# A longer planned landing time for cache pages in the second layer of a decoder step

## The chip, the cores and the metric

The kernel runs on one core of a Trainium2 chip. A core has five engines that run side by side: PE multiplies matrices, DVE works element by element and reduces, ACT computes functions and copies, POOL does element work more slowly, and SP issues DMAs. Each takes its own instructions strictly in the order in which they stand in the program and waits on semaphores for the others. The metric is the device time of one execution in microseconds (us); lower is better. Three runs of the kernel before are given, and one more execution was profiled.

## What is computed

One inference step of a decoder with two layers, for a prompt of 512 tokens and for 8 samples of 8 new tokens each (576 columns in all), in float32. Layer 0 is a gated delta rule mixer. Between the layers, keys and values that both groups share are projected. Layer 1, the one that matters here, is differential attention. The prompt attends to itself; each sample attends to 1024 past positions, which lie in a cache of pages of 128 positions, and to its own 8 tokens. Cut to layer 1 and the cache:

```python
past = page_table.shape[1] * PAGE_SIZE                      # 8 pages of 128 for each sample
k_past = cache_k[page_table].reshape(db, past, DIFF_HEADS, 2 * DIFF_DH)
v_past = cache_v[page_table].reshape(db, past, DIFF_HEADS, DIFF_VH)

def diff_block(q, k, v, q_pos, k_pos, lam):
    s = jnp.einsum('bqhmd,bkhmd->bhmqk', q, k) * DIFF_DH ** -0.5
    s = jnp.where((k_pos[None, :] <= q_pos[:, None])[None, None, None], s, -jnp.inf)
    p = jax.nn.softmax(s, axis=-1)
    p = p[:, :, 0] - lam * p[:, :, 1]
    return jnp.einsum('bhqk,bkhe->bqhe', p, v)

def diff_mixer(...):
    q, z = jnp.split(h @ w_in, [DIFF_WIDTH], axis=-1)
    ...
    o = rms_norm(o, sub_gain) * (1.0 - lam_init)
    o = o * jax.nn.silu(z)
    return o @ w_out
```

The page table gives each of the 8 samples 8 pages, in any order among the 80 of the cache. So 64 key pages and 64 value pages are read, 512 KB each.

## The kernel before

**How the program comes about.** The source does not write its instructions down in their final order. It is a planner: each piece of work is a Python generator that yields, before each group of instructions, the engine it will use, an estimated cost, and what must be done first: names of results, or a free buffer (a `Room`). The planner (`Weave`, and `Second` for layer 1) keeps for every engine the estimated moment at which it is free. In `drive` it looks at all live pieces, takes the one that could start earliest (of equals, the one of lower rank), lets it write its instructions, and books the engine. The order thus made is the order in the program: `pin` ties PE, ACT, DVE, POOL and, in layer 1, SP to it.

DMAs are planned as well. `load` enters a transfer with an estimated time; `transfers` lets the queue run, and when a transfer is through it notes its name in `done` with a moment at which its result may be used: the end of the transfer plus `LATE` = 0.6 us. That line is the one that changes. The moment has no part in the program: on the chip each instruction waits on a semaphore for its data. It decides only which work stands ahead of which.

**The pages.** `Pages.loads` goes through 128 pages in a fixed sequence: the keys of three samples, then by turns the values of one sample and the keys of the sample three further on. There are five buffers (`PG` = 5). For each page it takes the next free buffer, has POOL copy the page number into it (L2471), has SP read that number (L2474) and issue the load (L2476). The load's name for the planner is `kpage` or `vpage` with the page's number.

**Who uses them.** `Sample2.keys` multiplies queries with the key pages on PE, two pages at a time (`px<-pg,qs` in the profile: 8 matmuls a page, which the profile records as 16), and frees each buffer after its page. `Sample2.softmax` makes the probabilities (`px<-C,sp` turns them). `Sample2.values` multiplies them with the value pages, again in pairs (`po<-pg,pTs`). In the text, key pages are k0 to k63 and value pages v0 to v63 by sample; "page 11" of a sample's values means the v page of that number.

**What stands between the pages on PE.** The attention of the prompt (`Prompt2`): for each of 8 heads, scores (`sc<-kT,qT`, with the mask `sc<-cmaskb,identb`) in three groups for four blocks of queries, then a maximum on DVE (L2709), exponentials on ACT (L2713), a combination on DVE (L2726), transposes on PE (`pt<-con_ident,pm`) and the product with the values (`pv<-vn,pts`). Further the last value projections and the z projection in tiles of 24 matmuls, 8 steps of 3 (`pq<-hhi,whi`, `pq<-hlo,whi`, `pq<-hhi,wlo`). A tile needs a bank of PSUM; ACT and DVE (L2222, L2224) empty it. The bank `pq` is there once; when the last prompt head is through, `pick` lets z tiles take `pt2`, `sc` or `pv` too.

Weights come in float32 (`wraw`), are cast on ACT (L2013) and split on POOL in two halves (L2018) into a high and a low part. After the last page come the end of the samples' attention (`samples_end`), the rest of z and the output projection (`out_second`), whose first four tiles are taken in the banks pq, px, px and po.

Line numbers of the kernel after are two higher in these places. Buffer numbers as in `pq_17438` tell one tile from the next in the same bank.

Of the kernel before, what the change touches and what calls it, by code (L numbers as in the profile page):

```python
# [253 lines left out]
class Weave:  # L254
# [76 lines left out]
    def transfers(self, until):  # L331

        while True:
            act = [q for q in self.queues.values() if q]
            rate = SHARED if len(act) > 1 else 1.0
            lands = self.clock + min(q[0][0] for q in act) / rate if act else math.inf
            comes = self.coming[0][0] if self.coming else math.inf
            t = max(self.clock, min(lands, comes))
            if t > until or t == math.inf:
                return  # L340
            for q in act:
                q[0][0] -= (t - self.clock) * rate
            self.clock = t
            if comes <= lands:
                _, _, q, us, name = self.coming.pop(0)
                self.queues[q].append([us, name])
            else:
                for q in act:
                    if q[0][0] < 1e-9:
                        self.done[q.pop(0)[1]] = t + LATE, None  # L350
                return

    def set(self, *name):
# [517 lines left out]
LATE = 0.6  # L871
# [30 lines left out]
LATER_ROOMS = "z", "z", "v", "scr", "scr"  # L902
LATER_AT = 3
SB = 3
HELD = 4
EV = 3
CH = 3
# [1115 lines left out]
def run_part(W, K, j, ps, half, ks, step=2, conds=lambda k: ()):  # L2023

    ks = list(ks)
    for i in range(0, len(ks), step):
        now = ks[i:i + step]
        yield "E", None, ("w", j), *[c for k in now for c in conds(k)]
        w = W.sets[j]
        for k in now:  # L2030
            for a, b in ((0, 0), (0, 1), (1, 0)):
                K.mm(out=ps[:, :HT], lhsT=w[a][:, k, :], rhs=(K.hhi, K.hlo)[b][:, k, half * HT:half * HT + HT],
                     start=(k == 0 and a + b == 0), stop=(k == 7 and a == 1))
# [750 lines left out]
def out_second(W, K):  # L2784
# [31 lines left out]
    def conds(half):  # L2816
        return lambda k: (("g", k, half),) + ((("gs", 1),) if half else ())
    held = []
    names = ["pq", "px", "px", "po", "sc", "sc", "pt2", "pv"]
    for (m, half), name in zip(order[:HELD], names):  # L2820
        yield None, 0, Room(name), *((("gs", 1),) if name in ("px", "po") else ())
        bank = getattr(K, name).tile([128, 512], F32, name=name), W.took[0]
        yield from run_part(W, K, 40 + m, bank[0], half, range(7), conds=conds(half))
        held.append(bank)
    for (m, half), bank in zip(order[:HELD], held):
        yield from run_part(W, K, 40 + m, bank[0], half, (7,), conds=conds(half))
        W.add(0, evac(m, half, bank))
        if half:
            W.leave(W.sets[40 + m][2])
    for i, (m, half) in enumerate(order[HELD:]):  # L2830
        name = names[(i + HELD) % 8]
        yield None, 0, Room(name)
# [125 lines left out]
def phase_b(K, ctx, past):  # L2958
# [4 lines left out]
    def pool(name, bufs):  # L2963
        return ctx.enter_context(tc.tile_pool(name=name, bufs=bufs))
# [6 lines left out]
    K.pg = pool("bpg", PG)  # L2971
    K.scr = pool("scr", SB)
    first = pool("b1", 1)
# [21 lines left out]
    K.wnext -= 1  # L2995
    for name, bufs in (("pp", 3), ("pt", 2), ("px", 2), ("po", 1), ("pg", PG), ("scr", SB), ("ch", CH), ("vch", EV), ("tk", 2), ("raw", 2),
                       ("w", 4), ("w2", 3), ("wx", 1), ("qs", 2), ("p", PB), ("pTs", 2), ("os", 1), ("C", 2), ("ls", 2), ("mx", 2),
# [205 lines left out]
```

## Time and profile before

| what | us |
|---|---|
| three runs | 1198.29, 1199.89, 1205.4 |
| median of the runs | 1199.89 |
| the profiled execution | 1203.46 |
| its span, first to last instruction | 1201.7 |
| first use of a key page on PE | at 835.8 |
| first use of a value page | at 900.8 |
| last use of a value page | begins at 1092.3 |

A row of the profile names a line of the source, an engine, an operation and the tiles it writes and reads. In a timeline the first two numbers are start and duration, then follows, in brackets, how long the engine sat idle before and what ended that. Matmuls are pipelined: their durations overlap, so what one costs PE is the distance from its start to the start of the next. A stretch by windows gives for each engine the busy time and the number of instructions, then the clock granted to PE (1.00 is full), the share of time in which the DMA engines were busy, and GB/s. In the list of waits a row says who waited for whom, how long in all, how often, and the longest.

### The profile page before, as it was taken

To read this page: it belongs to the slowest core of one execution; us is meant where nothing else is said; L and a number is where in the kernel's file an instruction comes from. 1 tells how busy PE (TensorE), PEld (TensorE's weight loads), DVE (VectorE), ACT (ScalarE), POOL (GpSimd) and SP (SyncE) were. 2 spreads that over 40 slices of the span, in tenths; PEclk is the share of its full clock that TensorE was granted. 3 is DMA by queue.
4 is the path that set the end of the run, shared out by engine and by line. 5 is a ranking of instruction groups with operands and counts; after the bars stand their busy time and mean duration, and the time that the engine had idled before them with its cause. 6 is when DMAs were issued, how large, how long until landed. Compare 5 with 4: busy or idle time off the path is not lost.

```text
span 1201.7 us, 33311 instructions
## 1 busy us (share of the span) xinstructions
PE 1147.5 (95%) x12819; PEld 1050.2 (87%) x12819; DVE 766.7 (64%) x2223; ACT 688.0 (57%) x1894; POOL 373.8 (31%) x720
## 2 busy tenths in 40 slices
PE   8999999999999999899989999999999999998998
PEld 6899899998989998899988989998997777777998
DVE  5667876767877876668635467487644555555542
ACT  4766768677776867576545243865435545543430
POOL 2432322241322323232122340656524223121241
PEclk8999999999999999999999999999999999999999
DMA  9786667676666566566958985322948998993243
GB/s 363 211 216 161 156 158 165 178 168 185 175 175 174 135 173 153 179 176 172 255 164 232 337 283 181 106 66 79 346 154 310 326 334 304 346 329 100 58 125 116
DMA packets 87935, 241.06 MB, mean 201 GB/s; under 512 B 14482, under 2 KB 28690, under 8 KB 87778
## 3 DMA queue, kind: packets, MB, share of 16 engines
q1 hardware_dynamic: 71650, 180.22, 43.4%
q0 software_dynamic: 16128, 58.73, 22.2%
q8 instruction: 101, 1.65, 0.6%
q14 instruction: 56, 0.46, 0.1%
HBM read 213.07 MB, written 25.84 MB: 199 GB/s over the span
## 4 chain that ended last, share of the span: by engine, by line
PE 61%; DMA 14%; ACT 8%; issue 7%; DVE 6%; POOL 2%; SPq 1%; POOLq 0%; DVEq 0%; ACTq 0%
PE pp L292 16%; PE pp L1922 10%; PE pc L292 6%; DMA whi<-wall 5%; PE px L1922 5%; PE pq L1922 5%; PE pt L292 3%; PE sc L1922 3%; PE pt L1922 2%; DMA pg<-cv 2%; PE pt L1927 2%; PE po L1922 2%; PE pa L292 2%; PE pv L1922 2%; DMA pg<-ck 2%
## 5 line engine op out<-in xcount | busy, mean ns | idle before, releaser
L2018 POOL TENSOR_TENSOR wlo<-wraw,whi 128x512 fp32r<-128x512 f32 x94 | 122.8, 1327 | 179.0 <-ACT whi L2013 169.4
L292 PE MATMUL pp<-hlo,whi 128*128 128x288 f32 x592 | 172.3, 311 | 0.0
L292 PE MATMUL pp<-hhi,whi 128*128 128x288 f32 x592 | 163.1, 296 | 0.0
L1922 PE MATMUL pp<-hhi,whi 128*128 128x288 f32 x432 | 132.5, 307 | 3.0 <-DVE x L1821 2.3
L1922 PE MATMUL pp<-hlo,whi 128*128 128x288 f32 x432 | 127.6, 296 | 2.0 <-DVE hlo L1847 1.6
L1922 PE MATMUL pp<-hhi,wlo 128*128 128x288 f32 x432 | 125.9, 296 | 0.9 <-POOL wlo L2018 0.6
L292 PE MATMUL pp<-hhi,wraw 128*128 128x288 f32 x576 | 124.8, 301 | 0.0
L292 PEld LDWEIGHTS pp<-hlo,whi 128*128 128x128 f32 x592 | 112.3, 190 | 1.9 <-issue 1.2
L292 PEld LDWEIGHTS pp<-hhi,whi 128*128 128x128 f32 x592 | 112.5, 190 | 0.6
L292 PE MATMUL pp<-hhi,wlo 128*128 128x288 f32 x592 | 104.1, 303 | 0.1
L292 PEld LDWEIGHTS pp<-hhi,wraw 128*128 128x128 f32 x576 | 94.6, 190 | 0.5
L1922 PEld LDWEIGHTS pp<-hhi,whi 128*128 128x128 f32 x432 | 81.4, 188 | 6.6 <-issue 5.3
L1128 DVE SCALAR_TENSOR_TENSOR y<-u,vec,y 128x600 f32<-128x600 f32 x96 | 82.9, 865 | 5.6 <-ACT y L1125 5.1
L292 PEld LDWEIGHTS pp<-hhi,wlo 128*128 128x128 f32 x592 | 84.7, 188 | 2.0 <-issue 1.2
L292 PE MATMUL pp<-hlo,wraw 128*128 128x288 f32 x288 | 84.3, 315 | 0.0
L1922 PEld LDWEIGHTS pp<-hlo,whi 128*128 128x128 f32 x432 | 81.5, 189 | 2.7 <-DVE hlo L1847 2.1
L1922 PEld LDWEIGHTS pp<-hhi,wlo 128*128 128x128 f32 x432 | 80.7, 188 | 1.3 <-POOL wlo L2018 0.8
L937 POOL DMA_DIRECT2D wlo<-wall x38 | 33.7, 887 | 125.8 <-ACT wlo L932 84.9
L2471 POOL COPY pg<-ptt 1x1 int32<-1x1 int32 x128 | 25.8, 206 | 142.3 <-PE px L1922 78.4
L2013 ACT CAST whi<-wraw 128x1024 fp32r<-128x1024 f32 x47 | 49.0, 1046 | 33.8 <-DMA wraw<-wall 9.5
L1922 PE MATMUL pq<-hhi,whi 128*128 128x288 f32 x192 | 61.8, 322 | 3.1 <-DVE x L2224 2.9
L1922 PE MATMUL pq<-hhi,wlo 128*128 128x288 f32 x192 | 57.1, 297 | 0.0
(512 smaller groups left out, 3150.8 us busy)
## 6 DMA issues: line engine op xcount, KB each, us to landing
pg<-ck SPq DMA_DIRECT2D x64, 512.0 KB, 5.4
pg<-cv SPq DMA_DIRECT2D x64, 512.0 KB, 5.2
wraw<-wall SPq DMA_DIRECT2D x49, 512.0 KB, 4.4
whi<-wall POOLq DMA_DIRECT2D x38, 512.0 KB, 6.3
wlo<-wall POOLq DMA_DIRECT2D x38, 512.0 KB, 6.0
wraw<-wall POOLq DMA_DIRECT2D x36, 512.0 KB, 5.9
araw<-ada SPq DMA_DIRECT2D x24, 512.0 KB, 5.2
araw<-ada SPq DMA_DIRECT2D x8, 1024.0 KB, 14.6
```

The source lines that it names most:

```text
L292: return self.K.nc.tensor.matmul(**kw)
L937: K.nc.gpsimd.dma_start(out=lo[:], in_=src, accum_op=ALU.add)
L1128: nc.vector.scalar_tensor_tensor(out=y[:, :YW], in0=u[:, j:j + YW], scalar=cw[j], in1=y[:, :YW], op0=ALU.mult, op1=ALU.add)
L1922: return self.K.nc.tensor.matmul(**kw)
L1927: return self.K.nc.tensor.transpose(**kw)
L2013: nc.scalar.copy(out=hi[:], in_=raw[:])
L2018: nc.gpsimd.tensor_sub(out=lo[:, q:q + 4], in0=raw[:, q:q + 4], in1=hi[:, q:q + 4].bitcast(F32))
L2471: nc.gpsimd.tensor_copy(out=e, in_=P.ptt[0:1, i:i + 1])
```

## The change

One constant is new, and the moment of use that `transfers` notes depends on the name of what landed. For a name that holds "page" it is the end of the transfer plus `SPARE` = 1.4 us, for all others plus `LATE` = 0.6 us as before. Only the loads of layer 1's cache pages have such names.

```diff
             else:
                 for q in act:
                     if q[0][0] < 1e-9:
-                        self.done[q.pop(0)[1]] = t + LATE, None
+                        name = q.pop(0)[1]
+                        self.done[name] = t + (SPARE if "page" in str(name[0]) else LATE), None
                 return
...
 SB = 3
+SPARE = 1.4
 HELD = 4
```

Each engine has as many instructions as before; one of the 16 z tiles takes the bank `pt2` where `sc` was taken. The order on PE is the same until the key pages are in use, and differs from there to the end of the z projection. The places that the prediction speaks of are shown there.

## The prediction

> **What bounds the kernel now.** I read the page first (busy shares, then the chain that ended last), then busy time by stage, then who waits for whom on PE in the paged stage, then PE's timeline there row by row. The page's busy row and its chain by engine:
>
> ```profile
> PE 1147.5 (95%) x12819; PEld 1050.2 (87%) x12819; DVE 766.7 (64%) x2223; ACT 688.0 (57%) x1894; POOL 373.8 (31%) x720
> PE 61%; DMA 14%; ACT 8%; issue 7%; DVE 6%; POOL 2%; SPq 1%; POOLq 0%; DVEq 0%; ACTq 0%
> ```
>
> PE is nearly always busy, so a reordering that adds no work can win only PE's waits. The change acts where cache pages are used. Three stretches (PE, PEld, DVE, ACT and POOL busy, then clock, DMA share, GB/s): the last key pages, the stage that mixes value pages, keys, prompt attention and the z projection, and the tail after the last page.
>
> ```profile
> 865.00:900.00 35.00, 35.00 (x411) 33.87 (x410) 13.55 (x44) 13.48 (x26) 9.36 (x29) 1.00 0.51 178
> 900.00:1092.00 192.00, 183.89 (x2680) 146.36 (x2682) 100.79 (x303) 100.53 (x292) 48.99 (x139) 1.00 0.91 320
> 1092.00:1202.00 110.00, 100.61 (x744) 95.99 (x744) 51.44 (x132) 32.79 (x78) 29.19 (x22) 0.98 0.29 87
> ```
>
> Before 900 PE does not idle at all; from 900 to 1092 it idles 8.1 us, in the tail 9.4 us. Its waits, in the paged stage and then in the tail (us in all, times, longest):
>
> ```profile
> PE po L1922 <- DMA pg<-cv: 4.0, 7, 1.2
> PE px L1922 <- DMA pg<-ck: 1.6, 3, 0.7
> PE po L1922 <- POOL pg L2471: 0.8, 2, 0.4
> PE px L1922 <- POOL pg L2471: 0.6, 1, 0.6
> ...
> PE pq L1922 <- DVE x L2224: 2.6, 2, 2.3
> PE px L1922 <- DVE hlo L2665: 2.2, 1, 2.2
> ```
>
> The first four rows are all waits for a page (POOL's copy is a step of the same load): 4.0 + 1.6 + 0.8 + 0.6 = 7.0 us in 13 waits of about half a us. A page's loop is: PE ends with a buffer, POOL copies the page number, SP issues, the page lands, PE uses it. One step of it from the trace, issue to landing of the 128 pages:
>
> ```profile
> DMA to landing us min/median/max: 3.7/5.2/8.0
> ```
>
> With a copy of 0.17 us and about 1 us until SP issues it, a page takes some 6.5 us from release to landing. There are five buffers, so what decides is the PE work that the order puts between the last use of page n-5 and the first use of page n.
>
> **The change, part by part.** It adds no instruction to any engine. It tells the planner that a page lands 1.4 us after its transfer instead of 0.6, so a page's use sorts 0.8 us later and other ready PE work goes ahead of it. Loads of weights keep 0.6. The order is the same up to the key pages and differs from there to the last projection.
>
> First place, PE around value pages 12 to 15 of the second sample. Before (po<-pg is a pair of pages; pt2 transposes values, px<-C turns probabilities):
>
> ```order
> L1922 MATMUL po<-pg,pTs 8x128 x16
> L1927 MATMUL pt_14403<-con_ident,vch 128x128 x4
> L1922 MATMUL px<-C,sp 128x64 x8
> L1927 MATMUL pt_14451<-con_ident,vch 128x128
> L1922 MATMUL po<-pg,pTs 8x128 x16
> ```
>
> Now, from that last single transpose to the same pair:
>
> ```order
> L1929 MATMUL pt_14457<-con_ident,vch 128x128
> L1924 MATMUL sc<-kT,qT 128x128 x2
> L1924 MATMUL sc<-kT,qT 128x256 x2
> L1924 LDWEIGHTS identb
> L1924 MATMUL sc<-cmaskb,identb 128x128
> L1924 LDWEIGHTS identb
> L1924 MATMUL sc<-cmaskb,identb 128x128
> L1924 LDWEIGHTS identb
> L1924 MATMUL sc<-cmaskb,identb 128x128
> L1924 LDWEIGHTS identb
> L1924 MATMUL sc<-cmaskb,identb 128x128
> L1924 MATMUL po<-pg,pTs 8x128 x16
> ```
>
> A group of prompt scores moved ahead of the pair; one pair earlier, four k steps of z instead of two follow pages 10 and 11, and the score group of 512 columns moved in front of them. PE's timeline gives the prices, as start-to-start differences:
>
> ```profile
> 940.60 0.62 PE L1922 MATMUL po<-pg,pTs 128*8 128x128 f32 x16
> 941.44 0.62 PE L1922 MATMUL po<-pg,pTs 128*8 128x128 f32 x16 [0.21 <-DMA pg<-cv]
> 941.99 1.13 PE L1922 MATMUL sc<-kT,qT 64*128 64x512 f32 x4
> 943.15 0.38 PE L1922 MATMUL pq<-hhi,whi 128*128 128x288 f32 x1
> 944.13 1.06 PE L1922 MATMUL po<-pg,pTs 128*8 128x128 f32 x32
> 945.12 0.66 PE L1927 MATMUL pt<-con_ident,vch 128*128 128x128 f32 x4
> 945.61 1.90 PE L1922 MATMUL px<-C,sp 128*128 128x64 f32 x16
> 947.34 0.28 PE L1927 MATMUL pt<-con_ident,vch 128*128 128x128 f32 x1
> 947.55 0.62 PE L1922 MATMUL po<-pg,pTs 128*8 128x128 f32 x16
> 948.60 0.62 PE L1922 MATMUL po<-pg,pTs 128*8 128x128 f32 x16 [0.43 <-POOL pg L2471]
> 949.63 0.93 PE L1922 MATMUL sc<-kT,qT 64*128 64x128 f32 x8
> 950.72 0.39 PE L1927 MATMUL po<-con_ident,os 128*128 128x128 f32 x2
> 954.23 0.38 PE L1922 MATMUL pq<-hhi,whi 128*128 128x288 f32 x1
> 955.91 1.05 PE L1922 MATMUL pv<-vn,pts 128*128 128x128 f32 x8
> ```
>
> Page 15 goes into the buffer of page 10. Between the two PE has, before: page 11 (0.55), scores (943.15 - 941.99 = 1.16), two z steps (0.98), a pair (0.99), four transposes (0.49), px<-C (1.73), one transpose (0.21), page 14 (0.5): 6.6 us, and the wait of 0.43 at 948.60 is what was missing. Now: page 11 (0.55), four z steps (955.91 - 954.23 = 1.68), the transposes (0.49), the pair (0.99), px<-C (1.73), a transpose (0.21), the score group (950.72 - 949.63 = 1.09), page 14 (0.5): 7.2 us. So 0.6 us more stands there, just more than the wait.
>
> I summed both whole orders with such prices (0.133 us a projection matmul, 0.5 a page, 0.11 a transpose, 0.22 each matmul of pv<-vn and px<-C, 0.08 for a change of form) for the 104 pages from the first value page on. Work between release and use: mean 8.65 us before, 9.35 now; under 7.0 us at 29 pages before, at 12 now. What is missing to 7.0 us adds up to 15.9 us before and 5.2 now; to 6.5 us, 4.2 and 1.3. Both bounds leave about a third. Of 7.0 us of page waits 2.2 stay: **-4.8 us**. Ends: none removed (each page used later also frees its buffer later), 0; all removed, -7.0.
>
> Later use stretches the paged stage but fills it: after the last page 258 z matmuls were left, now 210, and the last prompt head is through; by the prices the tail falls from 98.2 to 85.0 us and the stage before it grows by 14.1. This moves work and gains nothing by itself.
>
> Second place, PE in the tail, where one z tile ends and the next begins. Before:
>
> ```order
> L1922 MATMUL pq_17438<-hhi_100,whi_16920 128x288
> L1922 MATMUL pq_17438<-hlo_101,whi_16920 128x288
> L1922 MATMUL pq_17438<-hhi_100,wlo_16921 128x288
> L1922 MATMUL pq_17496<-hhi_100,whi_16920 128x288
> L1922 MATMUL pq_17496<-hlo_101,whi_16920 128x288
> ```
>
> Now, at the first such handover of the tail:
>
> ```order
> L1924 MATMUL pq_17478<-hhi_100,whi_16729 128x288
> L1924 MATMUL pq_17478<-hlo_101,whi_16729 128x288
> L1924 MATMUL pq_17478<-hhi_100,wlo_16730 128x288
> L1924 MATMUL pt2_17567<-hhi_100,whi_16879 128x288
> L1924 MATMUL pt2_17567<-hlo_101,whi_16879 128x288
> ```
>
> Both tiles went through the single pq bank, so PE waited for ACT and DVE to empty it; now the last head is done before, the bank pt2 is free, and the tiles alternate. Four of PE's waits over 2 us, then the 4 us behind each (the clock is the third number from the right):
>
> ```profile
> 510.19 0.58 PE L292 MATMUL pt<-UL 128*128 128x128 f32 x2 [2.28 <-ACT UL L1717]
> 605.02 0.22 PE L292 MATMUL pa<-WC,V 32*32 32x32 f32 x2 [2.09 <-ACT V L1640]
> 1107.36 0.40 PE L1922 MATMUL pq<-hhi,whi 128*128 128x288 f32 x1 [2.26 <-DVE x L2224]
> 1149.53 0.40 PE L1922 MATMUL px<-hlo,whi 128*128 128x288 f32 x1 [2.18 <-DVE hlo L2665]
> 510.00:514.00 4.00, 3.81 (x17) 3.81 (x18) 2.37 (x9) 4.00 (x16) 1.79 (x5) 0.57 0.66 99
> 606.00:610.00 4.00, 4.00 (x25) 3.44 (x24) 1.12 (x4) 0.90 (x3) 2.06 (x3) 0.57 0.99 201
> 1108.00:1112.00 4.00, 4.00 (x17) 2.69 (x17) 1.00 (x4) 0.00 (x0) 0.00 (x0) 0.60 0.02 6
> 1149.00:1153.00 4.00, 3.47 (x26) 3.47 (x27) 3.35 (x9) 0.71 (x2) 0.00 (x0) 1.00 0.41 135
> ```
>
> The wait of 2.26 us goes: **-2.3 us** (ends 0 and -2.6). Three of the four were followed by a slow clock; two more waits as long, earlier in this layer, had none, so a wait does not suffice, but inside the span no slow stretch stands without one. Behind this wait it costs 4 us x (1 - 0.60) = 1.6 us. I take **-1.6**, since it goes with its wait; the other end is 0. The Trainium skill (TensorE: Matmul & The Clock Gate, Part 1) says that the clock halves after an idle window of about 3.4 us that runs freely; by that alone a wait of 2.26 us need not halve it, the slow stretch could have another cause and stay, and the sum would be 1.6 us less. The three rows at 0.57 to 0.60 behind waits of 2.1 to 2.3 us speak for the wait.
>
> The last wait stays: the last z tile must pass ACT and DVE before px can start its second half. Now that tile is in pq, which the output projection needs next, so PE stops there first; both stops lie under that one chain, so only its length counts: 0.
>
> POOL and SP: page copies and page loads keep their own sequence; weight splits (1.3 us a half) and weight loads stand elsewhere between them, one tile more within the paged stage. Cover: the copy has some 2 us per page. Ends 0 and the rival below.
>
> Additions: 11 more changes of form x 0.08 = **+0.9 us**. New small waits in a new order, two of half a us as the page waits have them: **+1.0** (ends 0 and +4).
>
> Sum: -4.8 - 2.3 - 1.6 + 0.9 + 1.0 = -6.8 us. The profiled execution took 1203.46 us (span 1201.7 and 1.8 around it), 3.6 above the median of 1199.89; it becomes 1196.7, and the median **1193.1 us**.
>
> **The rivals.** (a) The waits pass to the softmax of prompt attention. More of it runs between pages, and DVE and ACT need time between scores and transposes. For the widest group:
>
> ```profile
> L2709 DVE TENSOR_REDUCE mx<-sc 128x1 f32<-128x512 f32 x14 | 9.5, 686 | 8.3 <-PE sc L1922 8.3
> L2713 ACT ACTIVATE pm<-sc,mx 128x512 f32<-128x512 f32 x14 | 9.6, 687 | 9.8 <-DVE mx L2709 9.8
> L2726 DVE SCALAR_TENSOR_TENSOR pm<-pm,cf,pm 128x512 f32<-128x512 f32 x7 | 5.3, 751 | 0.2
> ```
>
> Maximum, two exponentials, combination: 0.69 + 2 x 0.69 + 0.75 = 2.8 us, some 3.7 with the short steps between. By my sum the least PE work in between was 6.2 us and is now 4.9, so it fits unless DVE is a us behind. If each of eight heads waits 0.6 us, +4.8: 1197.9.
>
> (b) Slower: page copies queue on POOL behind weight splits. POOL is in order, and a split waits for its weight, whose allowance stayed short:
>
> ```profile
> 903.33 4.96 POOL L2018 TENSOR_TENSOR wlo<-wraw,whi 128x512 fp32r<-128x512 f32 x4 [1.21 <-ACT whi L2013]
> 908.24 0.50 POOL L2471 COPY pg<-ptt 1x1 int32<-1x1 int32 x3
> ```
>
> Here four splits held POOL from 903.33 to 908.24, and four page copies went out at once behind them. A page has 8.65 - 6.5 = 2.1 us to spare on the mean, so PE sees up to 4.96 - 2.1 = 2.8 us of such a hold. Third place, POOL's order in the middle of the paged stage, before:
>
> ```order
> L2471 COPY pg<-ptt 1x1 x12
> L2495 COPY qs_9876<-qT 64x4x8 x4
> L2500 MEMSET sp 128x64
> L2471 COPY pg<-ptt 1x1 x5
> L2018 TENSOR_TENSOR wlo<-wraw,whi 128x512
> L2471 COPY pg<-ptt 1x1
> L2018 TENSOR_TENSOR wlo<-wraw,whi 128x512
> ```
>
> Now:
>
> ```order
> L2473 COPY pg<-ptt 1x1 x13
> L2020 TENSOR_TENSOR wlo<-wraw,whi 128x512
> L2497 COPY qs_9876<-qT 64x4x8 x4
> L2020 TENSOR_TENSOR wlo<-wraw,whi 128x512
> L2473 COPY pg<-ptt 1x1
> L2502 MEMSET sp 128x64
> L2473 COPY pg<-ptt 1x1 x15
> ```
>
> Two split halves moved ahead of the copy of page 61, with a sample's query copies between them. The gain is gone at three such holds, 8.4 us; at four the time is 1193.1 + 11.2 = 1204.3. Against it: POOL is busy 49 of 192 us.
>
> (c) Page waits do not shrink, since a later use frees its buffer later: 1193.1 + 4.8 = 1197.9, with the tail's gain lost too 1201.8. Against it: the order itself has the work in between.
>
> (d) All waits at page and bank go and nothing new comes: -7.0 - 2.6 - 1.6 + 0.9 = -10.3, 1189.6; the short gaps that the idle column does not count could add 3 us, 1186.6.
>
> **How the numbers follow.** The forecast (1190.5 to 1197) 0.45; (a) and (c), up to 1202, 0.27; (d), 1186.5 to 1190.5, 0.13; (b) 0.11; beyond these 0.04. The range 1186.5 to 1203 leaves out (b) and what lies beyond, 0.15. A measurement tells about 1% (12 us) from no change: below 1187.9 lies part of (d), 0.07; above 1211.9 a bad case of (b), 0.04; the same 0.89.
>
> **What would show it.** Right: page waits of PE near 2 us instead of 7.0, with the last page used some 10 us later and the tail as much shorter; no wait of 2 us at a z handover and no slow clock near it; PE's busy time unchanged. Wrong: page waits as before (c); waits of PE for ACT pm or DVE pm of several us (a); idle time of POOL's copies put down to a split, and landings late behind it (b).

## The result, and the profile after

| what | before | after |
|---|---|---|
| median of 20 runs each, us | 1201.99 (1195.81 to 1208.78) | 1193.71 (1187.02 to 1197.84) |
| ratio after / before, 95% interval | | 0.9922 [0.9904, 0.9939] |
| profiled execution, us (span) | 1203.46 (1201.7) | 1193.57 (1191.8) |
| first use of a key page on PE, at | 835.8 | 836.0 |
| first use of a value page, at | 900.8 | 900.5 |
| last use of a value page ends, at | 1092.6 | 1100.1 |
| from there to the end | 109.1 | 91.7 |

The kernel is faster by 0.78%, 9.4 us [7.3, 11.5]. This is worked out from all the runs; the two medians differ by 8.3 us. In the profiles all of the gain lies behind the first use of a key page. The page's busy row and the chain of the kernel after:

```profile
PE 1144.6 (96%) x12819; PEld 1051.5 (88%) x12819; DVE 764.5 (64%) x2223; ACT 687.4 (58%) x1894; POOL 373.0 (31%) x720
PE 65%; DMA 13%; ACT 8%; DVE 6%; issue 5%; POOL 2%; SPq 1%; POOLq 0%; DVEq 0%; ACTq 0%
```

The chain has four points more of PE and two less of "issue": the same work with fewer gaps. The three stretches of the prediction, by windows (PE, PEld, DVE, ACT, POOL busy, clock, DMA share, GB/s):

```profile
865.00:900.00 35.00, 35.00 (x432) 33.14 (x430) 13.29 (x43) 14.00 (x26) 10.08 (x30) 1.00 0.60 209
900.00:1092.00 192.00, 188.36 (x2689) 152.82 (x2687) 109.12 (x330) 106.11 (x312) 51.37 (x141) 1.00 0.91 312
1092.00:1202.00 110.00, 92.45 (x737) 89.76 (x735) 41.62 (x105) 26.35 (x56) 25.89 (x20) 0.99 0.32 97
```

In the paged stage PE is busy for 188.36 us where it was 183.89; idle time fell from 8.1 to 3.6 us. The tail's row runs past the end of the program (the span ends at 1191.8). PE's waits, first up to 1100, then behind:

```profile
PE po L1924 <- DMA pg<-cv: 1.4, 3, 0.6
PE px L1924 <- DMA pg<-ck: 1.2, 3, 0.6
PE pq L1924 <- DVE x L2226: 0.6, 1, 0.6
PE pt L1929 <- ACT vch L2236: 0.5, 1, 0.5
PE pt L1929 <- DVE qT L2773: 0.5, 1, 0.5
PE pt L1929 <- DVE pm L2728: 0.2, 1, 0.2
...
PE pq L1924 <- DVE x L2226: 1.7, 2, 1.0
PE px L1924 <- DVE hlo L2667: 0.9, 1, 0.9
```

Waits for pages went from 7.0 us in 13 to 2.6 in 6 (2.7 with one of 0.1 us that the list leaves out); these six are all for a landing (DMA), none for POOL's copy. In the tail the waits of 2.26 and 2.18 us are gone; three short ones stand there, from PE's timeline:

```profile
1110.63 0.40 PE L1924 MATMUL pq<-hhi,whi 128*128 128x288 f32 x1 [0.66 <-DVE x L2226]
1135.51 0.40 PE L1924 MATMUL pq<-hhi,whi 128*128 128x288 f32 x1 [1.05 <-DVE x L2226]
1139.64 0.40 PE L1924 MATMUL px<-hlo,whi 128*128 128x288 f32 x1 [0.94 <-DVE hlo L2667]
```

The first is a handover between z tiles. The other two are what became of the last wait: the output projection stops once for the bank pq and once for the last z tile, 1.05 + 0.94 = 1.99 us in place of 2.18.

### The profile page after: what moved, and what is told of

Its sections match the earlier page's. It is cut to its first block, busy times and chain, and to the rows that moved or that the text cites. A ratio compares the mean times of both kernels' runs of the same rounds, so it can differ in the third digit from the quotient of the medians.

```text
span 1191.8 us, 33310 instructions
## 1 busy us (share of the span) xinstructions
PE 1144.6 (96%) x12819; PEld 1051.5 (88%) x12819; DVE 764.5 (64%) x2223; ACT 687.4 (58%) x1894; POOL 373.0 (31%) x720
## 4 chain that ended last, share of the span: by engine, by line
PE 65%; DMA 13%; ACT 8%; DVE 6%; issue 5%; POOL 2%; SPq 1%; POOLq 0%; DVEq 0%; ACTq 0%
PE pp L292 19%; PE pp L1924 9%; PE pc L292 6%; PE pq L1924 5%; PE px L1924 5%; DMA whi<-wall 3%; PE sc L1924 3%; PE pt L1929 3%; PE po L1924 2%; PE pa L292 2%; PE pt L1924 2%; PE pt L292 2%; DMA pg<-cv 2%; PE pv L1924 2%; DMA qT<-ada 2%
## 5 line engine op out<-in xcount | busy, mean ns | idle before, releaser
L1924 PE MATMUL pp<-hhi,wlo 128*128 128x288 f32 x432 | 127.2, 299 | 1.0 <-POOL wlo L2020 0.6
L292 PE MATMUL pp<-hhi,wlo 128*128 128x288 f32 x592 | 105.3, 305 | 1.4 <-issue 1.2
L1924 PE MATMUL pq<-hlo,whi 128*128 128x288 f32 x192 | 56.5, 294 | 0.0
```

Of the source, the lines that this page charges most:

```text
L292: return self.K.nc.tensor.matmul(**kw)
L1924: return self.K.nc.tensor.matmul(**kw)
```

## The experiments

**Page waits alone.** Two kernels load only a quarter of each page, so that a page lands sooner; orders stay as they were before and after. PE reads the two heads that are there in place of all eight, so what comes out for the samples is not the layer's result.

```diff
-                nc.sync.dma_start(out=t[:], in_=cache[bass.ds(r, 1)].rearrange("a p (h t) -> p (a h) t", h=8))
+                nc.sync.dma_start(out=t[:, 0:2], in_=cache[bass.ds(r, 1)].rearrange("a p (h t) -> p (a h) t", h=8)[:, 0:2])
...
-                            K.mm(out=S[32 * j:32 * j + 32, o:o + 128], lhsT=qs[:, h, :], rhs=kp[:, h, :],
+                            K.mm(out=S[32 * j:32 * j + 32, o:o + 128], lhsT=qs[:, h, :], rhs=kp[:, h % 2, :],
...
-                        K.mm(out=po[32 * j:32 * j + 8, hf, :], lhsT=self.pTs[:, pg, 8 * h:8 * h + 8], rhs=vp[:, h, :],
+                        K.mm(out=po[32 * j:32 * j + 8, hf, :], lhsT=self.pTs[:, pg, 8 * h:8 * h + 8], rhs=vp[:, h % 2, :],
```

In the order of before:

> The kernel before, in its own order, but each page load brings only two of the eight heads (128 KB instead of 512 KB) and PE reads these two heads in place of all eight; PE has as many matmuls as before, and what comes out for the samples is not the reference's. Theory (page waits cost the time): PE's waits for pages, 7.0 us of idle before, fall under 1 us and the kernel gets 7 to 10 us faster, to about 1192 to 1195; the wait of over 2 us where one z tile follows the other in the bank pq stays. Rival (the tail made the gain): at most 3 us faster. Rival (a different order as such made it): no change, since the order is the same.

In the order of after:

> The changed kernel, in its own order, with the same short page loads (two of eight heads, so the samples' results are not the reference's). Theory: the 2.6 us of page waits that are left go, 2 to 4 us faster than the changed kernel, about 1190 to 1192; against the other kernel with short loads it is 2 to 5 us faster, which is the part of the tail (bank handover, 2.3 us, and slow clock, 1.6 us). Rival (the gain is page waits alone): as fast as the other one with short loads, within 1 us. Rival (the tail alone): 6 us or more faster than the other one.

Measured: 1187.89 us (ratio to before 0.9867 [0.9829, 0.9904]) and 1189.11 (0.9868 [0.9831, 0.9905]). No wait for a page is left in either. What PE waits for up to the last page, in the order of before with quarters:

```profile
PE pt L1927 <- ACT vch L2234: 0.5, 1, 0.5
PE pq L1922 <- DVE x L2224: 0.3, 1, 0.3
```

The first kernel gained more than the theory's 7 to 10 us. The second was to be 2 to 5 us faster than the first and is 1.2 us slower, so by the runs the rival came (page waits alone make the gain). By the profiles it did not. From the first key page to the end, first in the order of before, then in that of after, both with quarters:

```profile
834.40:1191.50 357.10, 346.99 (x4242) 305.00 (x4241) 185.53 (x550) 162.54 (x421) 104.96 (x231) 0.99 0.35 107
831.10:1183.00 351.90, 343.61 (x4243) 303.03 (x4241) 183.83 (x550) 161.52 (x421) 102.99 (x232) 1.00 0.35 109
```

The second is 5.2 us shorter there, with 2.5 us less of waits in the tail and 3.1 us less of slow clock. The six runs of each spread over 9 and 7 us and don't settle it; the tail is tested by itself below.

The stretch from the first to the last use of a value page, by windows, in the kernel before (whole pages):

```profile
900.80:1092.60 191.80, 183.69 (x2687) 146.13 (x2686) 100.72 (x304) 100.61 (x292) 48.99 (x139) 1.00 0.90 319
```

The same stretch in a second execution of before:

```profile
901.00:1093.80 192.80, 183.47 (x2687) 145.99 (x2685) 100.84 (x304) 100.88 (x292) 48.36 (x139) 1.00 0.91 318
```

In the order of before with quarters:

```profile
899.40:1080.90 181.50, 180.47 (x2687) 147.06 (x2687) 101.11 (x304) 100.93 (x293) 49.90 (x139) 1.00 0.39 117
```

In the kernel after (whole pages):

```profile
900.50:1100.10 199.60, 195.19 (x2787) 158.79 (x2786) 111.74 (x335) 108.84 (x319) 51.37 (x141) 1.00 0.90 308
```

And in the order of after with quarters:

```profile
895.50:1091.20 195.70, 193.99 (x2787) 159.10 (x2785) 111.61 (x335) 109.06 (x319) 51.23 (x141) 1.00 0.36 111
```

The same 2687 instructions take PE 191.8 and 192.8 us with whole pages and 181.5 with quarters: 10.3 and 11.3 us for page waits that the list gives as 7.0 and 8.2. The rest is in the busy column, 183.6 against 180.5: some 3 us that count as work and vanish with the waits. In the order of after the stretch loses 3.9 us, and the busy column 1.2. So page waits cost about half as much again as the list of waits says.

The traces show where that part sits. With PE's instructions of before and of its twin with quarters matched one by one, 10.2 of the 10.3 us lie at the matmuls on pages and 0.1 at all others, so fewer bytes do not make PE faster in general. Without a wait the second page of a pair starts 0.09 us after the last matmul of the first. With one it starts 0.27 us plus the listed idle time after it, because idle time is counted from the end that the profile gives to that matmul. So a listed wait between two pages is 0.18 us longer than it looks (at 948.60, 0.61 us where the list has 0.43). Twelve of before's thirteen waits are of this kind, 2.2 us; most of the rest stands at pages whose wait is too short for the list.

Timed, the quarters in the order of before gain 16 us [11.6, 20.6], of which the stretch explains 10 to 11; they also take two thirds of the traffic away, and the rest isn't resolved.

**Other allowances.** Only the number changes, to 0.8, 1.6 and 2.0 us.

```diff
-SPARE = 1.4
+SPARE = 0.8
```

> The changed kernel with the allowance 0.8 us instead of 1.4. By the sums over its order the PE work between a page's release and its next use is 8.83 us on the mean (8.65 before, 9.35 with 1.4), and what is missing to 7 us adds up to 18.0 us (15.9 and 5.2). Theory: page waits of 6 to 9 us on PE, time as before within 4 us (1198 to 1206). Rival (any new order with some allowance helps): 4 us or more faster than before.

Measured: 1197.96 us, ratio 0.995 [0.9914, 0.9985]; page waits 3.7 us in 8, tail waits 3.0. Two tenths of a us more than before already bring some 60% of the gain (0.50 of 0.78%, with wide intervals). So the rival came and the theory did not: by the count in the order 18.0 us are missing to 7.0, more than the 15.9 of before, and yet PE waits half as long for pages. The wait at the first z handover is gone here too, as in after.

> An allowance of 1.6 us instead of 1.4. By the order only 4 of 104 pages have less than 7.0 us of work (12 at 1.4), mean 9.94 us, 1.3 us missing to 7.0. Theory (page waits are what the change gains, and fewer are better): no page wait over 0.3 us, page waits under 1 us, and the time 2 to 4 us under after, near the kernel of before with small pages (1188). Rival (as at 2.0 us, where no page wait was left and the time was not below after's): 1194 to 1197, since the later use makes other waits or the clock decides.

Measured: 1196.65 us, ratio 0.9939 [0.9908, 0.9969]: not below after. Instead of less than 1 us there are 4.7 us of page waits in this execution, 3.7 of them in two:

```profile
974.80 0.62 PE L1924 MATMUL po<-pg,pTs 128*8 128x128 f32 x16 [1.55 <-DMA pg<-cv]
1007.23 0.62 PE L1924 MATMUL po<-pg,pTs 128*8 128x128 f32 x16 [2.15 <-DMA pg<-cv]
```

Both pages took 6.7 to 7.0 us from issue to landing (5.4 on the mean), and POOL's copy for the first came 1.32 us after PE's last matmul on its buffer began, against 0.7 on the mean. The order gives the work in between; it doesn't give the time that a page needs, which scatters.

> The changed kernel with the allowance 2.0 us. Sums over its order: 9.99 us of PE work on the mean between release and next use, 0.6 us missing to 7 us in all; but four z tiles follow each other in the bank pq with less than 1.3 us between, 4.2 us missing (3.6 before, 1.3 with 1.4). Theory: page waits under 1 us, 1 to 2 us less than with 1.4, and 2 to 4 us more of waits for the bank pq: the time is that of the changed kernel within 4 us. Rival (later is always better): 4 us or more faster than with 1.4. Rival (later costs, since buffers come free later): slower than with 1.4 by 4 us or more.

Measured: 1195.77 us, ratio 0.9934 [0.9893, 0.9975]. No wait for a page is left, and the 2 to 4 us more of waits for the bank pq did not come either (1.9 us in all). Yet it isn't faster than after: the last wait (px for DVE hlo) is whole again with 2.17 us, and a slow stretch follows it. Beyond 1.4 us of allowance these runs show nothing more won.

**The parts of the change.** The longer allowance for value pages alone, then for key pages alone (the same edit with "kpage"):

```diff
-                        self.done[name] = t + (SPARE if "page" in str(name[0]) else LATE), None
+                        self.done[name] = t + (SPARE if "vpage" in str(name[0]) else LATE), None
```

> The longer allowance for value pages alone. By the order, the mean work between release and use is 8.98 us (before 8.65, after 9.35), 21 of 104 pages have less than 7.0 us (29, 12), and 10.8 us are missing to 7.0 (15.9, 5.2); to 6.5 it is 2.2 (4.2, 1.3). Theory (the gain comes from page waits, of which it removes those that the counts say): page waits of 4 to 5 us instead of 7.0, and half of the gain of after: ratio to before about 0.996. Rival (a value page's use that is put off holds its buffer, and the key page that takes it next comes late): page waits of 6 or more, mostly at key pages, and no gain.

> The longer allowance for key pages alone. By the order, mean work 8.73 us, 20 pages under 7.0 us, 10.7 us missing to 7.0 and 3.9 to 6.5: by 7.0 as good as value pages alone, by 6.5 as before. Theory: page waits of 5 to 7 us, most at value pages as before, and less gain than with value pages alone: ratio to before 0.996 to 1.000. Rival (the two parts are equal, each half of the change): the same ratio as the value pages alone, 0.996.

Measured: value pages 0.9939 [0.9907, 0.997], key pages 0.9983 [0.9957, 1.001]; together -0.78%, as the whole change. Both intervals hold the rival's 0.996. The waits behind the last page, with value pages alone (those with key pages alone are before's, 2.6 and 2.2):

```profile
PE pq L1924 <- DVE x L2226: 1.1, 1, 1.1
PE px L1924 <- DVE hlo L2667: 0.9, 1, 0.9
```

Page waits differ little, 3.4 and 4.4 us, both less than the theory had. What sets the two apart in the profiles is the tail: 2.1 us of waits with value pages alone, 5.1 with key pages alone. Only the value pages move so much work ahead of the last page that the last prompt head is through at the first handover. So by the profiles the rival (both halves equal) falls; by the runs alone it is only the less likely.

**The tail alone.** In the kernel after, no second bank:

```diff
-        yield from take(W, K, pick(W, "pq", "pt2", "sc", "pv") if kind == "z" and ("pv", 7, 3) in W.done else name)
+        yield from take(W, K, name)
```

> The kernel after, but every z tile keeps to the bank pq, as the first tiles of the tail did in the kernel before. Nine handovers in the tail then go through one bank, where before had one with a wait of 2.26 us and after has two short ones (1.7 us in all). My prediction's theory: each costs PE about 2.3 us, so nine cost some 20 us of waits, 18 more than after; if a slow clock of 1.6 us followed each wait, as the prediction assumed for one, another 14 us: 1212 to 1226 against 1194 of after. Rival: the wait is as long but the slow stretches come at other times and as often as elsewhere: time up by 16 to 20 us, granted clock of the runs .993 as before. Second rival: PE's queue and the other work hide most of a handover: time within 5 us of after.

Measured: 1205.3 us, ratio to before 1.0042 [1.0014, 1.0069], so by the two ratios 14 us above after. Nine handovers wait 10.4 us, not 20. Their first two and the last in PE's timeline:

```profile
1112.91 0.61 PE L1924 MATMUL pq<-hhi,whi 128*128 128x288 f32 x1 [2.31 <-DVE x L2226]
1120.44 0.40 PE L1924 MATMUL pq<-hhi,whi 128*128 128x288 f32 x1 [0.99 <-DVE x L2226]
...
1152.57 0.40 PE L1924 MATMUL pq<-hhi,whi 128*128 128x288 f32 x1 [1.05 <-DVE x L2226]
```

A bare handover costs 1.0 us; the first costs 2.31 because DVE came late to empty the tile. Four rows of DVE's timeline there:

```profile
1109.94 0.16 DVE L171 TENSOR_TENSOR rat<-ray 128x4 f32<-128x4 f32 x1
1110.13 1.14 DVE L172 TENSOR_TENSOR rat<-rat,rah 128x4 f32<-128x4 f32 x1
1111.31 1.19 DVE L173 SCALAR_TENSOR_TENSOR ray<-rat,ray 128x4 f32<-128x4 f32 x1
1112.42 0.44 DVE L2226 SCALAR_TENSOR_TENSOR x<-scr,pq 128x288 f32<-128x288 f32 x1
```

POOL's timeline has one row beside them:

```profile
1109.99 2.48 POOL L2020 TENSOR_TENSOR wlo<-wraw,whi 128x512 fp32r<-128x512 f32 x2 [16.06 <-ACT whi L2015]
```

In the profile the stretch behind the last page is 14.7 us longer than in after (106.4 for 91.7): 9.2 of idle time, 5.8 of slow clock, -0.2 of the rest. The slow clock is one stretch of 10.24 us at 1108.6, which costs 5.1 us, and one at the very end, which costs 0.7; none follows the eight waits of 1 us. The first of them lies around the long wait but began 2 us ahead of it, so that wait can't have started it. The measured time lies between the theories: a handover costs PE, but 1 us each.

Then the kernel before with a second bank and nothing else:

```diff
-        yield from take(W, K, pick(W, "pq", "pt2", "sc", "pv") if kind == "z" and ("pv", 7, 3) in W.done else name)
+        yield from take(W, K, pick(W, "pq", "pt2", "sc", "pv") if kind == "z" and ("pv", 7, 0) in W.done else name)
```

> The kernel before, whose allowance stays 0.6 us, but z tiles may take a second bank once the first block of the last prompt head is through instead of the last: the first handover of the tail goes from pq to sc, as it went from pq to pt2 after the change. The order on PE is the same up to that handover, so the page waits stay 7 us. Prediction's theory: the wait of 2.26 us falls below 0.7 and the slow clock behind it goes, in all 2 to 4 us: 1198 to 1200 against some 1202, ratio 0.9967 to 0.9984; the last wait of 2.2 us (px for DVE hlo) and its own slow clock stay. Rival (the bank part is worth nothing: the head's last scores now wait, or the slow clock comes elsewhere): ratio 0.999 to 1.001, with a new wait of about 2 us in the tail.

Measured: 1200.97 us, ratio 0.997 [0.9948, 0.9993]: 3.6 us [0.8, 6.3] for the bank alone, as the theory had it. One wait is left in the tail:

```profile
PE px L1922 <- DVE hlo L2665: 2.2, 1, 2.2
```

The same edit with quarter pages:

> The kernel of before with small page loads (2 of 8 heads of each page, 128 KB; results of the samples' attention not the reference's) and the same second bank in the tail. Without it this kernel took 1187.9, with the order of after 1189.1. Theory (page waits and tail waits add up): 2 to 4 us below the small pages alone: 1184 to 1186, no page wait, tail idle 3 us instead of 5.2. Rival (the tail part is worth nothing in timed runs, as the two kernels with small pages suggested): 1187 to 1189.

Measured: 1183.99 us, ratio 0.9845 [0.9809, 0.9882], against 0.9867 [0.9829, 0.9904] without: the direction of the theory, though the intervals overlap. In the two profiles the stretch from the first key page to the end is 5.0 us shorter with the second bank. With quarter pages in the order of after, whose tail waits are short as well, the ratio was 0.9868, which speaks for the rival. So with quarter pages the runs don't resolve the tail's worth; the kernel with whole pages and the second bank does.

**Both kernels once more.**

> The kernel after once more, unchanged, for a second profiled execution. Theory: waits at the same places as in the first (page waits 2 to 4 us, tail waits 2.6 us, none above 1.1), no slow clock in the tail since no wait of 2 us is there, ratio to before 0.990 to 0.994. Rival for the clock (slow stretches come by chance wherever): one or two in the tail this time.

> The kernel before once more, unchanged, for a second profiled execution. Theory: the two tail waits of 2.26 and 2.18 us at the same places, each followed by a slow stretch of 3.4 us in about two of three cases; page waits 6 to 8 us. Rival for the clock: the slow stretches stand elsewhere in the tail. Rival for the page waits (they scatter from one execution to the next): below 5 or above 9 us.

Measured: after 1190.18 us, ratio 0.9907 [0.987, 0.9944]; before 1206.39 in its one run. Waits of PE in before's second execution, up to 1100 and behind:

```profile
PE po L1922 <- DMA pg<-cv: 3.7, 5, 1.7
PE px L1922 <- DMA pg<-ck: 3.5, 4, 1.5
PE po L1922 <- POOL pg L2471: 1.0, 3, 0.4
...
PE pq L1922 <- DVE x L2224: 2.6, 2, 2.2
PE px L1922 <- DVE hlo L2665: 2.2, 1, 2.2
```

and in after's second:

```profile
PE po L1924 <- DMA pg<-cv: 0.9, 2, 0.6
PE px L1924 <- DMA pg<-ck: 0.6, 1, 0.6
...
PE pq L1924 <- DVE x L2226: 1.7, 2, 1.0
PE px L1924 <- DVE hlo L2667: 0.9, 1, 0.9
```

The tail's waits repeat to a tenth of a us. Of before's page waits ten of twelve stand at the same pages in both executions, so the order sets the place; but their sizes differ by up to four times (0.24 and 0.98 us at page 47 of the values). Executions with before's order up to the tail had 7.0, 8.2 and 5.0 us of them (the last is the kernel with the second bank alone), those with after's 2.7, 1.6 and 2.8 (the last is the kernel without it): 6.7 and 2.4 on the mean. The second executions lie just outside what was expected of them (8.2 for 6 to 8, 1.6 for 2 to 4).

The clock is decided by these runs too. Before, second execution: its two long waits in PE's timeline:

```profile
1108.65 0.40 PE L1922 MATMUL pq<-hhi,whi 128*128 128x288 f32 x1 [2.24 <-DVE x L2224]
1150.88 0.40 PE L1922 MATMUL px<-hlo,whi 128*128 128x288 f32 x1 [2.18 <-DVE hlo L2665]
```

The same execution by windows, behind each of them (the clock is the third number from the right):

```profile
1110.50:1113.50 3.00, 3.00 (x8) 1.15 (x8) 0.59 (x1) 0.00 (x0) 0.00 (x0) 0.50 0.02 5
1151.50:1154.50 3.00, 3.00 (x15) 3.00 (x14) 2.20 (x6) 0.71 (x2) 0.00 (x0) 0.50 0.38 142
```

After, first execution, by windows behind its two waits of about 1 us:

```profile
1135.00:1139.00 4.00, 3.19 (x22) 2.96 (x22) 3.93 (x5) 3.38 (x9) 3.34 (x3) 1.00 0.55 164
1139.00:1143.00 4.00, 3.36 (x25) 3.36 (x26) 3.45 (x9) 0.71 (x2) 0.00 (x0) 1.00 0.47 139
```

Fourteen executions were profiled. Leaving out the kernel with one bank, their tails hold 13 waits of 2.17 to 2.73 us. Nine were followed within 1.6 us by a slow stretch of 3.41 us at half clock, which costs 1.7 us; four were not. Of 28 waits of 0.9 to 1.7 us from the first key page on, in all fourteen, none was, nor one of 2.15 among the pages. Apart from the program's last 4 us and the one stretch of the kernel with one bank, no slow stretch stands there without a long wait. The rival (chance) falls for this part of the program.

There is no sharp limit at 2 us, though. The same traces have many waits of PE ahead of the first key page. From 30 us on, a slow stretch began between the wait's start and 1.6 us behind its end at 1 of 40 waits of 0.9 to 1.4 us, at 9 of 60 of 1.4 to 2.0, at 9 of 14 of 2.0 to 2.4, and at 17 of 22 longer ones. So the chance grows with the length of the wait.

## Why the prediction came out as it did

The time, 1193.71 for 1193.1, is closer than the sum, by luck: the gain was 9.4 us [7.3, 11.5] where the sum had 6.8. The three runs shown had a median of 1199.89, twenty have 1201.99, and these 2.1 us hide most of what the sum lacked. Term by term:

- *Page waits, -4.8.* By the list 6.7 became 2.4 on the mean, -4.4, so for these two orders the count of work between release and use gave the right mean. It is no measure that carries: at 0.8 us of allowance it had 18.0 us missing and PE waited 3.7, at 1.6 us it had 1.3 and PE waited 4.7. The prediction took the loop of a page as 6.5 to 7.0 us throughout, with about 1 us from POOL's copy to SP's issue. In before's trace that step takes 1.3 us at the median, and the loop, from the end of PE's last matmul on the buffer to the landing, 7.2 us at the median and 4.9 to 11.7 in all (90 pages whose landing the trace tells). That this spread is why the count fails is not shown. The list, too, holds too little. With quarter pages PE's busy column fell by some 3 us in the order of before and by 1.2 in that of after, so another 2 us belong to this term, about -6.4 in all. The value-page stretch with whole pages less the one with quarters says the same: 10.3, 11.3 and 9.0 us in three executions with before's order, 3.9, 2.9 and 4.7 in three with after's. The wait at page 15 of the values, 0.43 us in the prediction's example, came again with 0.42 in before's second execution and in neither of after's.
- *Handover between z tiles, -2.3.* 2.26 us became 0.66; another 0.3 us at a later handover went as well: -1.9. The bank alone, with its clock, gave 3.6 us [0.8, 6.3]; the prediction's two terms for it had 3.9.
- *Last wait, 0.* Two stops of 1.99 us in all where one of 2.18 was: right in length.
- *Slow clock, -1.6.* **This is the step that failed, in size.** The mechanism holds, but not for one wait only: the prediction let the last wait stay, as far as the clock goes, and did not see that cutting it into 1.05 and 0.94 takes its slow stretch away too. Two waits, each followed in 9 of 13 cases by 1.7 us: -2.4 on the mean; in the four profiles 1.7 and 3.4 us behind these waits before, none after. Its remark that no slow stretch in the span stands without a wait of about 2 us overlooked one of 6.83 us at 12.1, with only a wait of 0.7 us ahead of it. The rule weighed there, that the clock halves after an idle window of about 3.4 us that runs freely (the Trainium skill, TensorE: Matmul & The Clock Gate, Part 1), agrees with slow stretches of 3.41 us or a multiple; that a wait of 2.2 us would leave the clock alone was not so in nine cases.
- *Changes of form, +0.9, and new small waits, +1.0.* PE's time without waits and slow clock, from the first key page to the end, is 350.0 us on the mean before and 348.6 after, three executions each (the same as for the page waits). That is 1.4 less, of which page waits hidden in the busy column are 2: so the changes of form cost 0.6 or less. With quarter pages they cost nothing that shows (347.5 and 346.7, then 347.2). New small waits are 0.6 us (other waits of the paged stage 1.1 before, 1.7 after, in the first profiles), and a wait of 0.3 us for DVE pm in the tail went.

Measured terms: -6.4 - 1.9 - 0.2 - 2.4 + 0.6 + 0.6 - 0.3 = -10.0, within the interval of the runs and close to the difference of the two profiles (10.1 us from the first key page on). That it fits to a tenth is luck: the terms are in part means over several executions, and the second executions of the two kernels differ by 14.3 us there.

Of the rivals, (a) did not come: PE waits 0.2 us for DVE pm. (b) did not come: the long hold of POOL by four splits is there as before, and PE has no page wait near it; at 1.6 us of allowance a late copy stood ahead of a wait. POOL's timeline in after:

```profile
903.99 4.97 POOL L2020 TENSOR_TENSOR wlo<-wraw,whi 128x512 fp32r<-128x512 f32 x4 [2.19 <-ACT whi L2015]
908.89 0.41 POOL L2473 COPY pg<-ptt 1x1 int32<-1x1 int32 x3
```

Rival (c) is refuted: page waits shrank in each execution. (d), all waits gone, was not reached: 7 us of waits are left behind the first key page, though the gain comes near its 10.3 us. That the last page is used later and the tail is shorter came as forecast: 7.5 us later and 17.4 shorter, where 10 and 13.2 + 2.3 + 1.6 = 17.1 were worked out.

Open: whether the late copies at 1.6 us are what keeps a longer allowance from paying. A sixth page buffer, and a longer allowance for the weights too, were not tried. No version tried with whole pages is faster than after.

## What to carry to other kernels

When a planner's landing time is too short, count in the order how much work stands between a buffer's release and its next use, and compare its whole spread with the loop of release, issue and landing; both scatter. Here the mean gain came out for the one change and not for two other allowances, and the size of a single wait never did. Try more than one allowance: 1.6 and 2.0 us gained no more here than 1.4. Much of the effect may sit elsewhere: more than a third came from a bank that was free earlier and from waits cut short enough that no slow clock followed. Compare terms with the same order and less data before trusting the idle column, since it gave a third too little.

## What the runs showed of the hardware

- Waits of PE of about 2.2 us cost more than their length: in the tail 9 of 13 were followed by 3.41 us at half clock, and from the first key page on none of 28 of 0.9 to 1.7 us. Ahead of it the chance grows with the length, from 1 of 40 (0.9 to 1.4 us) to 17 of 22 (2.4 us or more). One stretch of 10.24 us, in the kernel with one bank, began 2 us ahead of a wait of 2.31; its start stays unexplained.
- PE's busy column can hold waiting: 2687 instructions in the same order took 183.6 us beside whole pages and 180.5 beside quarters. A wait between two pages on PE is 0.18 us longer than the idle time listed for it.
- The part ahead of the first key page has the same order in all fourteen executions, yet its slow stretches cost 3.4 to 13.7 us. In the twenty runs of after, time and mean granted clock go together (correlation -0.85), so slow clock makes most of their scatter.
- Two DVE steps on 128x4 elements took 1.14 and 1.19 us instead of 0.16 while POOL split a weight beside them (rows above), about the length of one split (2.48 us for two). The fourteen traces have 1134 steps of these three lines: all 18 that took over 0.3 us overlapped a split, and of the 1107 that met none the longest took 0.22. No run moved the splits to test it. The Trainium skill (GPSIMD Engine Reference, Specifications) says that POOL's interface to SBUF is shared with VectorE and contended for by DVE instructions with two SBUF inputs; these rows agree with it.
